# A hybrid attention and GLA layer: decays one head ahead, a modulation inside attention, a gate projection and the blocks of queries in other places

## The chip, the cores and the metric

The kernel runs on one core of a Trainium2 chip. The metric is the device time of one execution in microseconds (us). Several runs of the kernel are timed, and the profile is of one more execution. PE is the matrix engine, DVE, ACT and POOL are the vector, scalar and GpSimd engines, SP issues the transfers (DMA).

## The reference

One layer over 1024 latent tokens of width 1024 in fp32, with 256 context tokens. Cut to what matters:

```
h = modulate(rms_norm(x), shift1, scale1)          # adaLN: 6 vectors of 1024, silu(c) @ w_ada
k, v, gla k, gla v, low rank, q, gla q, gla gate, gate_a, gate_g = split(h @ w_in)
attention: 8 query heads, 2 key/value heads, qk norm, rotary, softmax over 1024 + 256 keys
g = log_sigmoid(lowrank @ w_gk + b) / 16           # decays, per head and direction
gla: S_t = diag(exp(g_t)) S_(t-1) + k_t^T v_t ;  o_t = q_t S_t    # forward and backward, 4 heads
y = sigmoid(gate_a) * (attn @ w1) + sigmoid(gate_g) * (gla @ w2)
x = x + gate1 * (y @ w_out)                        # gate1 is vector 2 of the six
out = x + gate2 * mlp(modulate(rms_norm(x), shift2, scale2))      # vectors 3, 4, 5
```

## The kernel before

Every large product is split into high and low parts and run as three matmuls (`mm3`, L171 to L175), so PE has most of the work. The program is a sequence of stages. Each is written as Python generators, and `merge(main, filler, n_main)` (L40) runs a main generator and fills it with the steps of projection GEMMs, spread evenly. A tile scheduler then sets each engine's order; each engine works its own queue in that order, and all transfers are issued from SP's one queue in order. Buffers come from rings: S 19, G 16, m1 10, m2 6, small ty 14.

The stages in time: a prologue (norm, the first two modulation vectors); `context()` (the 256 context tokens); `gla(0)` to `gla(3)`, each with projections as fillers; the projections of k and q for attention, where each one's norm, rotation and transposes (its *tail*, L850) is merged with the next one's GEMM; attention; the merge of the branches; the output projection; the MLP.

Within `gla(h)` come, in this order, the decays (`decays`, L435: four PSUM tiles of 512 columns, then Abs, Exp and Ln on ACT and subtractions on DVE), one cumulative scan per direction (L645, L647), the *level stage* (seven levels: differences of the scans at L673 and L674, L677 and L678, Exp at L675 and L679, multiplications by q and k at L683 and L685, 32-wide block products on PE at L631), a preparation, and the *chunk loop* (L722: eight steps i, two directions, where PE's L732 and L734 read and feed the state that DVE updates at L736).

`modulation()` (L1084) computes the other four modulation vectors from a 1024x4096 weight; `along` (L57) runs it step by step beside the fillers that are marked `M(...)` at L912 to L915:

```
for i in range(4):
    raw = self.m2(shape=(P, 2, 256))
    nc.sync.dma_start(raw, a["w_ada"][i * 256:(i + 1) * 256, c0:c0 + 256].rearrange("(k p) c -> p k c", p=P))
    for k in range(2):
        sk = self.silu[:, 2 * i + k, 0:1]
        if i == 0 and k == 0:
            nc.vector.tensor_scalar(acc, raw[:, k, :], sk, None, op0=ALU.mult)
        else:
            nc.vector.scalar_tensor_tensor(acc, raw[:, k, :], sk, acc, op0=ALU.mult, op1=ALU.add)
```

Attention (L954) goes over 16 blocks of 128 queries of one key/value group, four heads each. While a block's probabilities are transposed (L996), split by ACT (L190) and DVE (L191) and multiplied with the values (`values`, L1011), the next block's scores run (`scores`, L963), with maxima on DVE (L975 to L980) and exponentials on ACT (L987, L988). The first block's scores are merged with the last gate projection, `pg(1, 3)`, and with the last query tail (L1044 to L1052). `kv_load` (L929) loads the keys and values of a group, `q_load` (L940) the queries of a block.

## Time and profile before

| | |
|---|---|
| three runs | 2148.75, 2148.76, 2155.94 us; median 2148.76 us |
| profiled execution | 2144.9 us; span of the trace 2143.0 us |
| granted clock of PE, mean over the span | 0.980 of full speed |
| busy time over the span | PE 94%, DVE 69%, ACT 47%, POOL 30% |

The profiled execution is one of its own and not among the three runs. A busy share is an average over stages; which engine is waited for differs from stage to stage. Times in the trace are counted from the span's start. "Busy" of matmuls is modelled, and a granted clock below 1 in a stretch means that PE ran part of it at the lower of its two levels.

### The profile page before, as it was taken

To read this page: it belongs to the slowest core of one execution; us is meant where nothing else is said; L and a number is where in the kernel's file an instruction comes from. 1 tells how busy PE (TensorE), PEld (TensorE's weight loads), DVE (VectorE), ACT (ScalarE), POOL (GpSimd) and SP (SyncE) were. 2 spreads that over 40 slices of the span, in tenths; PEclk is the share of its full clock that TensorE was granted. 3 is DMA by queue.
4 is the path that set the end of the run, shared out by engine and by line. 5 is a ranking of instruction groups with operands and counts; after the bars stand their busy time and mean duration, and the time that the engine had idled before them with its cause. 6 is when DMAs were issued, how large, how long until landed. Compare 5 with 4: busy or idle time off the path is not lost.

```text
span 2143.0 us, 32673 instructions
## 1 busy us (share of the span) xinstructions
PE 2018.4 (94%) x12526; PEld 1688.6 (79%) x12526; DVE 1482.1 (69%) x2216; ACT 999.8 (47%) x1783; POOL 634.7 (30%) x408
## 2 busy tenths in 40 slices
PE   4999898998999999789999998999699999999999
PEld 2898687887878999578888776877588887788887
DVE  6533787769668578577777678857756547788784
ACT  3354545435254223266666544336555556344341
POOL 2100322322331222100000356202423235475470
PEclk9999999999999999999999999999899999999999
DMA  8243431331524323461111367664153547644441
GB/s 290 64 121 120 134 99 37 104 106 37 157 64 156 112 79 140 159 184 45 35 55 40 122 215 246 220 215 143 44 177 134 186 143 240 212 157 157 138 153 64
DMA packets 230140, 284.13 MB, mean 133 GB/s; under 512 B 19376, under 2 KB 156736, under 8 KB 229984
## 3 DMA queue, kind: packets, MB, share of 16 engines
q1 hardware_dynamic: 229920, 281.91, 40.5%
q8 instruction: 99, 1.62, 0.3%
q0 software_dynamic: 64, 0.13, 0.1%
q14 instruction: 57, 0.47, 0.1%
HBM read 200.18 MB, written 81.81 MB: 132 GB/s over the span
## 4 chain that ended last, share of the span: by engine, by line
PE 51%; DVE 4%; DMA 1%; issue 1%; ACT 1%; POOL 0%; SPq 0%; DVEq 0%; ACTq 0%; POOLq 0%
PE p L173 8%; PE p L175 8%; PE p L174 8%; PE g L175 5%; PE g L173 5%; PE g L174 5%; PE b L996 3%; PE b L173 2%; PE b L175 2%; PE b L174 2%; PE s L173 2%; PE s L175 1%; PE s L174 1%; DVE G L1155 1%; DVE W L1128 0%
## 5 line engine op out<-in xcount | busy, mean ns | idle before, releaser
L173 PE MATMUL g<-whi,S 128*128 128x256 f32 x896 | 259.9, 290 | 0.0
L175 PE MATMUL g<-whi,S 128*128 128x256 f32 x896 | 253.4, 283 | 0.0
L174 PE MATMUL g<-wlo,S 128*128 128x256 f32 x896 | 252.7, 282 | 0.0
L1128 DVE TENSOR_TENSOR W<-Q,W 128x512 fp32r<-128x512 f32 x160 | 130.9, 822 | 101.3 <-ACT W L1127 101.0
L173 PE MATMUL p<-S,W 128*128 128x512 f32 x384 | 155.1, 404 | 20.1 <-ACT W L1127 18.2
L173 PEld LDWEIGHTS g<-whi,S 128*128 128x128 f32 x896 | 170.9, 191 | 1.8 <-issue 0.4
L174 PEld LDWEIGHTS g<-wlo,S 128*128 128x128 f32 x896 | 170.9, 191 | 1.0
L175 PEld LDWEIGHTS g<-whi,S 128*128 128x128 f32 x896 | 170.6, 190 | 0.3
L1127 ACT CAST W<-R 128x512 fp32r<-128x512 f32 x152 | 93.9, 620 | 149.5 <-PE p L175 105.7
L161 POOL TENSOR_TENSOR wlo<-wraw,whi 128x1024 fp32r<-128x1024 f32 x32 | 92.8, 2918 | 232.9 <-ACT whi L160 231.5
L175 PE MATMUL p<-S,W 128*128 128x512 f32 x384 | 154.0, 402 | 2.0 <-DVE W L1128 2.0
L174 PE MATMUL p<-S,W 128*128 128x512 f32 x384 | 154.2, 402 | 0.0
L1128 DVE TENSOR_TENSOR W<-R,W 128x512 fp32r<-128x512 f32 x152 | 139.5, 921 | 21.2 <-ACT W L1127 21.1
L175 PE MATMUL p<-G,W 128*128 128x512 f32 x384 | 152.0, 396 | 0.1
L174 PE MATMUL p<-G,W 128*128 128x512 f32 x384 | 152.0, 396 | 0.0
L1175 POOL TENSOR_TENSOR Q<-R 128x512 f32<-128x512 f32 x40 | 60.3, 1509 | 309.5 <-DVE W L1128 214.8
L173 PE MATMUL p<-G,W 128*128 128x512 f32 x384 | 151.9, 396 | 0.0
L1127 ACT CAST W<-Q 128x512 fp32r<-128x512 f32 x160 | 98.5, 621 | 110.7 <-PE g L175 51.1
L191 DVE TENSOR_TENSOR G<-b,G 128x512 fp32r<-128x512 f32 x164 | 111.8, 686 | 48.0 <-ACT G L190 47.7
L173 PE MATMUL g<-S,whi 128*128 128x512 f32 x336 | 139.0, 414 | 6.0 <-ACT S L268 6.0
L175 PE MATMUL g<-S,wlo 128*128 128x512 f32 x336 | 135.1, 402 | 0.8 <-POOL wlo L161 0.8
L1155 POOL TENSOR_TENSOR S<-S 128x512 fp32r<-128x512 f32 x38 | 53.9, 1420 | 274.1 <-ACT S L1154 204.9
(339 smaller groups left out, 5561.7 us busy)
## 6 DMA issues: line engine op xcount, KB each, us to landing
R<-in_w_mlp_dram SPq DMA_DIRECT2D x32, 1024.0 KB, 6.2
wraw<-in_w_in_dram SPq DMA_DIRECT2D x60, 512.0 KB, 4.0
u<-S SPq DMA_DIRECT2D x96, 256.0 KB, 2.9
m<-in_w_ada_dram SPq DMA_DIRECT2D x64, 256.0 KB, 4.2
G<-u SPq DMA_DIRECT2D x64, 256.0 KB, 3.8
S<-u SPq DMA_DIRECT2D x48, 256.0 KB, 3.6
G<-in_w_ada_dram SPq DMA_DIRECT2D x16, 512.0 KB, 10.5
R<-in_w_out_dram SPq DMA_DIRECT2D x8, 1024.0 KB, 7.4
```

The lines of the kernel that those rows point to most:

```text
L161: self.lo_engine.tensor_tensor(lo[:, s, :], raw, hi[:, s, :].bitcast(F32), op=ALU.subtract)
L173: nc.tensor.matmul(out, lh, rh, start=first, stop=False, skip_group_check=more)
L174: nc.tensor.matmul(out, lh, rl, start=False, stop=False, skip_group_check=more)
L175: nc.tensor.matmul(out, ll, rh, start=False, stop=last, skip_group_check=more)
L191: self.nc.vector.tensor_tensor(lo, src, hi.bitcast(F32), op=ALU.subtract)
L996: nc.tensor.transpose(pt[:, h * P:(h + 1) * P], src, self.ident)
L1127: self.nc.scalar.copy(hi, v)
L1128: self.nc.vector.tensor_tensor(lo, v, hi.bitcast(F32), op=ALU.subtract)
L1155: (engine or self.nc.vector).tensor_tensor(b[:, 1, :], v, b[:, 0, :].bitcast(F32), op=ALU.subtract)
L1175: tt(s[0], a21, a22, op=ALU.add)
```

## The change

- `decays` becomes a generator that stops after each of its four tiles. A new `sums_of_decays(h)` runs it and scans in place. Head h+1's is stepped from head h's chunk loop, from i=2 on; head 0's is at the end of `context()`. `gla(h)` only fetches the result.
- `modulation()` leaves the fillers and is stepped once for each block of attention from the second on. It now loads 32 tiles of 128x1024 into S buffers, multiplies them on ACT (`scalar.mul`) and adds them on POOL, where before it took 128 operations of 128x256 on DVE and 64 loads.
- `pg(1, 3)` is merged with the last query tail, ahead of attention, whose first scores now run alone.
- The blocks of queries are taken in another order, and the loads of the second group, of the modulation and of the GLA outputs are issued behind the latest `q_load` (`issue_after`). The PSUM pool of attention takes over its banks tile by tile.

The diff, cut:

```diff
                 nc.vector.tensor_scalar(mn, p, bias, 0.0, op0=ALU.add, op1=ALU.min)
                 todo.append((s, mn))
+                yield
         for s, _ in todo:
             nc.scalar.activation(s, s, AF.Exp, scale=-1.0)
         for s, mn in todo:
             nc.scalar.activation(s, s, AF.Ln, bias=1.0)
             nc.vector.tensor_tensor(s, mn, s, op=ALU.subtract)
+        yield
...
-
-    CONTEXT_STEPS = 1 + 2 + 4 * 6 + 2 + 1
+        yield from self.sums_of_decays(0)
+
+    CONTEXT_STEPS = 1 + 2 + 4 * 6 + 2 + 1 + 7
...
-        b = []
-        gs = [self.G(), self.G()]
-        self.decays(h, self.lr, T, gs)
-        yield
...
-                nc.vector.tensor_tensor_scan(bt[:, ::-1], self.reset, g[:, ::-1], 0.0, op0=ALU.mult, op1=ALU.add)
-            b.append(bt)
-            yield
-        bf, bb = b
+        bf, bb = b = self.b.pop(h)
...
+        ahead = self.sums_of_decays(h + 1) if h < 3 else None
...
+                if h < 3 and i >= 2:
+                    next(ahead, None)
                 yield
         nc.vector.tensor_scalar(ss, ss, 1.0 / 256, EPS, op0=ALU.mult, op1=ALU.add)
         self.orstd[h] = self.rsqrt(ss, NT)
         self.o[h] = o
         yield
 
-    GLA_STEPS = 2 + 3 + 21 + 1 + 6 + 16 + 1
+    GLA_STEPS = 2 + 21 + 1 + 6 + 16 + 1
+
+    def sums_of_decays(self, h):
+
+        nc = self.nc
+        self.b[h] = b = [self.G(), self.G()]
+        yield from self.decays(h, self.lr, T, b)
+        for d in range(2):
+            r = slice(None, None, -1 if d else 1)
+            nc.vector.tensor_tensor_scan(b[d][:, r], self.reset, b[d][:, r], 0.0, op0=ALU.mult, op1=ALU.add)
+            yield
...
-            pg, md = self.proj_gate, self.modulation()
+            pg = self.proj_gate
...
-            M = lambda f: along(f, md, 6)
             merge(self.context(), [(4, lambda: self.fm_block(w1, 1, sink)), gv(0), pg(0, 1), pg(1, 2)], self.CONTEXT_STEPS)
...
-            merge(self.gla(0), [kq(1), pg(0, 2), M(gv(1))], self.GLA_STEPS)
-            merge(self.gla(1), [kq(2), go(0), pg(0, 3), M(gv(2))], self.GLA_STEPS)
-            merge(self.gla(2), [kq(3), go(1), pg(1, 0), M(gv(3))], self.GLA_STEPS)
-            merge(self.gla(3), [pg(1, 1), go(2), M(self.proj_v())], self.GLA_STEPS)
+            merge(self.gla(0), [kq(1), pg(0, 2), gv(1)], self.GLA_STEPS)
+            merge(self.gla(1), [kq(2), go(0), pg(0, 3), gv(2)], self.GLA_STEPS)
+            merge(self.gla(2), [kq(3), go(1), pg(1, 0), gv(3)], self.GLA_STEPS)
+            merge(self.gla(3), [pg(1, 1), go(2), self.proj_v()], self.GLA_STEPS)
...
                 merge(tail, [gemm], 10)
                 tail = nxt[1]() if nxt else iter(())
-            run_all(md)
+            merge(tail, [pg(1, 3)], 10)
             self.attention_loads()
-        return tail, pg(1, 3)
...
         for j in range(2):
-            self.move(q[j], self.qT[j][4 * kv:4 * kv + 4, :, qb * P:(qb + 1) * P].rearrange("h d t -> d h t"))
+            self.last_q = self.move(q[j], self.qT[j][4 * kv:4 * kv + 4, :, qb * P:(qb + 1) * P].rearrange("h d t -> d h t"))
...
+    def attention(self):
+        nc = self.nc
+        with self.psum_phase("pat", {"s": 2, "sc": 1, "b": 3}, "tile") as self.pp:
...
-                th = qb // 4
-                self.at[kv, th] = rb
-                if kv == 1:
-                    if th == 0:
-                        return
+                at = self.at.setdefault(qb % 4, {})
+                at[kv, qb // 4] = rb
+                if len(at) == 4:
                     t0 = qb % 4 * P
                     for t in range(2):
-                        self.operands(self.at, t, lambda i: self.atD[:, i, :, t0:t0 + P].rearrange("j d t -> d j t"), lambda r: r.rearrange("p (h t) -> p h t", t=P))
-
-            blocks = [(kv, q + 4 * th) for q in range(4) for kv in range(2) for th in range(2)]
+                        self.operands(at, t, lambda i: self.atD[:, i, :, t0:t0 + P].rearrange("j d t -> d j t"), lambda r: r.rearrange("p (h t) -> p h t", t=P))
+
+
+            blocks = [(0, 0), (0, 4), (0, 1), (1, 0), (1, 4), (0, 5), (1, 1), (1, 5)] + [(kv, q + 4 * th) for q in (2, 3) for kv in range(2) for th in range(2)]
...
-            def first():
-                for _ in scores(0, st):
-                    if st["todo"]:
-                        exponentials(st)
-                    next(tail, None)
-                    yield
-                run_all(tail)
-            self.lo_engine = nc.vector
-            merge(first(), [gate], 12)
+            for _ in scores(0, st):
+                if st["todo"]:
+                    exponentials(st)
+            if st["todo"]:
+                exponentials(st)
             self.close_wts.close()
             self.wts, self.close_wts = self.open("tw", side="right", reuse_waits="tile")
-            late = []
+            late, md = [], self.modulation()
             for n, (kv, qb) in enumerate(blocks):
                 nxt, sg = None, iter(())
-                if n == 0:
-                    kvs[1] = self.kv_load(1)
-                if n in (9, 11):
-                    self.load_blocks(self.glaD, n // 11)
                 if n + 1 < len(blocks):
                     nxt = start(n + 1)
                     sg = scores(blocks[n + 1][0], nxt)
+                with self.tc.issue_after(self.last_q.ins):
+                    if n == 0:
+                        kvs[1] = self.kv_load(1)
+                    if n > 0:
+                        next(md, None)
+                    if n in (9, 11):
+                        self.load_blocks(self.glaD, n // 11)
...
-            accs = []
-            for j in range(4):
-                c0 = (2 + v) * D + j * 256
-                acc = self.m1()
-                for i in range(4):
-                    raw = self.m2(shape=(P, 2, 256))
-                    nc.sync.dma_start(raw, a["w_ada"][i * 256:(i + 1) * 256, c0:c0 + 256].rearrange("(k p) c -> p k c", p=P))
-                    for k in range(2):
-                        sk = self.silu[:, 2 * i + k, 0:1]
-                        if i == 0 and k == 0:
-                            nc.vector.tensor_scalar(acc, raw[:, k, :], sk, None, op0=ALU.mult)
-                        else:
-                            nc.vector.scalar_tensor_tensor(acc, raw[:, k, :], sk, acc, op0=ALU.mult, op1=ALU.add)
-                accs.append(acc)
...
+            acc = self.S()
+            for k in range(KT):
+                raw = self.S()
+                nc.sync.dma_start(raw, a["w_ada"][k * P:(k + 1) * P, (2 + v) * D:(3 + v) * D])
+                sk = self.silu[:, k, 0:1]
+                if k == 0:
+                    nc.scalar.mul(acc, raw, sk)
+                else:
+                    nc.scalar.mul(raw, raw, sk)
+                    nc.gpsimd.tensor_tensor(acc, acc, raw, op=ALU.add)
+                if k % 4 == 3:
+                    yield
             p = self.ps("a")[:, :256]
             for j in range(4):
-                nc.tensor.matmul(p[32 * j:32 * j + 32, :], self.ones[:, 0:32], accs[j], start=True, stop=True, tile_position=(0, 32 * j))
+                nc.tensor.matmul(p[32 * j:32 * j + 32, :], self.ones[:, 0:32], acc[:, j * 256:(j + 1) * 256], start=True, stop=True, tile_position=(0, 32 * j))
             row = self.m1()
```

What it moves on three engines is shown as rows of each engine's order (line, operation, written tile, read tiles, shape; `a` and `g` are PSUM tiles, a number tells buffers of one name apart).

ACT in head 0, the decays of head 1 before: they stand together, after the chunk loop (L742 is its last operation).

```order
L448 ACTIVATE G_3151<-a_3153,vec 128x512
L448 ACTIVATE G_3151<-a_3159,vec 128x512
L448 ACTIVATE G_3152<-a_3165,vec 128x512
L448 ACTIVATE G_3152<-a_3171,vec 128x512
L453 ACTIVATE G_3151<-G_3151 128x512 x2
L453 ACTIVATE G_3152<-G_3152 128x512 x2
L455 ACT_TABLE_LOAD
L455 ACTIVATE G_3151<-G_3151 128x512 x2
L455 ACTIVATE G_3152<-G_3152 128x512 x2
```

All Exps run ahead of all Lns here, so one table load separates them.

ACT at the same decays after, inside head 0's chunk loop (L719 is the chunk loop's copy, L438 Abs, L444 Exp, L446 Ln). Exp and Ln alternate tile by tile, with a table load at each alternation; head 0's copies stand between them. Over the program the table loads grow from 17 to 35.

```order
L438 ACTIVATE G_2752<-a_2754,vec 128x512
L719 COPY G_2654<-a_2745 128x256
L444 ACTIVATE G_2752<-G_2752 128x512
L438 ACTIVATE G_2752<-a_2766,vec 128x512
L446 ACT_TABLE_LOAD
L446 ACTIVATE G_2752<-G_2752 128x512
L719 COPY G_2655<-a_2760 128x256
L444 ACT_TABLE_LOAD
L444 ACTIVATE G_2752<-G_2752 128x512
L446 ACT_TABLE_LOAD
L446 ACTIVATE G_2752<-G_2752 128x512
L438 ACTIVATE G_2753<-a_2804,vec 128x512
```

DVE at that place after (L440 is the bias and minimum, L447 the subtraction that takes Ln's result, L741 the scans, L717 the update of the state that the chunk loop's matmuls read).

```order
L447 TENSOR_TENSOR G_2752<-m_344_2758,G_2752 128x512
L447 TENSOR_TENSOR G_2752<-m_348_2770,G_2752 128x512
L717 SCALAR_TENSOR_TENSOR m_351_2801<-m_340_2749,ty_2564,a_2797 128x256
L741 SCALAR_TENSOR_TENSOR G_2752<-reset,G_2752 128x1024
L440 TENSOR_SCALAR m_353_2808<-a_2804,vec 128x512
L717 SCALAR_TENSOR_TENSOR m_355_2813<-m_346_2763,ty_2602,a_2810 128x256
L440 TENSOR_SCALAR m_357_2820<-a_2816,vec 128x512
L447 TENSOR_TENSOR G_2753<-m_353_2808,G_2753 128x512
L447 TENSOR_TENSOR G_2753<-m_357_2820,G_2753 128x512
L741 SCALAR_TENSOR_TENSOR G_2753<-reset,G_2753 128x1024
L717 SCALAR_TENSOR_TENSOR m_359_2851<-m_351_2801,ty_2564,a_2847 128x256
```

The updates of the state, which had stood among filler work, now stand between subtractions and scans; `m_359`, the state after step i=4 in one direction, is behind the second scan.

SP at the start of attention before (`q_hi` and `q_lo<-G` are the last query tail's stores, `G<-k_hi` begins `kv_load(0)`, `S_8984<-k_lo` is in `kv_load(1)`, `sgg<-S` are the last gate's stores, `S<-q_hi` the second block's queries).

```order
L122 DMA q_hi<-G_8626 128x1024
L122 DMA q_lo<-G_8627 128x1024
L122 DMA G_8690<-k_hi 128x1024
L122 DMA q_hi<-G_8669 128x1024
L122 DMA q_lo<-G_8670 128x1024
L122 DMA G_8691<-k_lo 128x1024
...
L605 DMA sgg<-S_8887 128x1024
L122 DMA S_8984<-k_lo 128x1024
...
L122 DMA S_8986<-v1l 128x4x128
L122 DMA S_8993<-q_hi 128x4x128
```

The first group's keys stand between the tail's stores, and the second block's queries last.

SP at the same place after.

```order
L112 DMA q_hi<-G_8521 128x1024
L112 DMA q_lo<-G_8522 128x1024
L598 DMA sgg<-S_8506 128x1024
L112 DMA q_hi<-G_8554 128x1024
L112 DMA q_lo<-G_8555 128x1024
L112 DMA G_8575<-k_hi 128x1024
L112 DMA G_8576<-k_lo 128x1024
...
L112 DMA G_8578<-v1l 128x4x128
L112 DMA S_8671<-q_hi 128x4x128
L112 DMA S_8671<-q_lo 128x4x128
L112 DMA S_8674<-k_hi 128x1024
```

The first group's loads went behind all of the tail's stores and the gate's, and the second block's queries went ahead of the second group's keys (`S_8674`).

## Rows read from the trace of the kernel before

**Rows 1.** The page, part 1: busy time, share and instructions.

```profile
PE 2018.4 (94%) x12526; PEld 1688.6 (79%) x12526; DVE 1482.1 (69%) x2216; ACT 999.8 (47%) x1783; POOL 634.7 (30%) x408
```

**Rows 2.** Stretches: length, busy PE, PEld, DVE, ACT, POOL, granted clock, DMA, GB/s.

```profile
240.00:300.00 60.00, 51.86 (x613) 41.34 (x612) 53.76 (x58) 32.15 (x42) 19.56 (x11) 0.91 0.23 73
355.00:405.00 50.00, 43.81 (x673) 39.43 (x672) 49.03 (x62) 26.50 (x36) 13.41 (x8) 0.97 0.14 43
485.00:530.00 45.00, 38.76 (x582) 35.91 (x583) 42.89 (x55) 20.57 (x27) 10.84 (x7) 0.92 0.12 37
615.00:655.00 40.00, 33.76 (x540) 30.47 (x538) 40.00 (x46) 18.26 (x24) 15.97 (x7) 0.96 0.17 54
...
850.00:940.00 90.00, 69.49 (x354) 54.98 (x354) 51.59 (x97) 33.45 (x70) 11.04 (x8) 0.92 0.67 199
...
940.00:1200.00 260.00, 260.00 (x1506) 216.78 (x1504) 197.79 (x406) 177.06 (x385) 21.97 (x17) 1.00 0.14 43
...
370.00:380.00 10.00, 5.88 (x97) 5.61 (x96) 10.00 (x10) 3.07 (x4) 5.04 (x2) 0.83 0.36 107
```

**Rows 3.** Waits: us in total, times, longest (240 to 700; last row 850 to 940).

```profile
PE a L631 <- DVE G L685: 26.2, 12, 5.1
...
PE a L732 <- DVE m L736: 5.8, 5, 2.5
...
PE s L173 <- DMA S<-q_hi: 6.2, 1, 6.2
```

**Rows 4.** DVE's timeline, second head: start, us, instruction, [idle before <- releaser].

```profile
350.02 2.50 DVE L456 TENSOR_TENSOR G<-m,G 128x512 f32<-128x512 f32 x4 [2.93 <-ACT G L455]
...
354.64 2.77 DVE L647 TENSOR_TENSOR_SCAN G<-reset,G 128x1024 f32<-128x1024 uint8 x1
...
369.74 3.10 DVE L683 TENSOR_TENSOR G<-G,G 128x1024 f32<-128x1024 f32 x1
372.76 3.36 DVE L685 TENSOR_TENSOR G<-G,G 128x1024 f32<-128x1024 f32 x1
...
381.31 1.21 DVE L685 TENSOR_TENSOR G<-G,G 128x1024 f32<-128x1024 f32 x1
```

**Rows 5.** ACT's timeline, first head's end and second head's decays.

```profile
319.86 0.37 ACT L738 COPY G<-a 128x256 f32<-128x256 f32 x1 [2.92 <-DVE m L736]
...
342.87 1.84 ACT L448 ACTIVATE G<-a,vec 128x512 f32<-128x512 f32 x3
...
345.86 2.18 ACT L453 ACTIVATE G<-G 128x512 f32<-128x512 f32 x4
348.06 1.28 ACT L455 ACT_TABLE_LOAD   x1
349.36 2.20 ACT L455 ACTIVATE G<-G 128x512 f32<-128x512 f32 x4
```

**Rows 6.** PE's timeline, two successive steps of the first head's chunk loop.

```profile
314.89 0.67 PE L732 MATMUL a<-m,G 128*128 128x256 f32 x2
...
319.98 0.67 PE L732 MATMUL a<-m,G 128*128 128x256 f32 x2
```

**Rows 7.** Groups by line (240 to 700; L1009 950 to 1200; L675 whole span).

```profile
L736 DVE SCALAR_TENSOR_TENSOR m<-m,ty,a 128x256 f32<-128x256 f32 x53 | 25.1, 477 | 44.7 <-PE a L734 38.3 <-DMA m<-in_w_ada_dram 6.3
...
L1009 ACT COPY m<-b 128x512 f32<-128x512 f32 x13 | 7.7, 593 | 0.9 <-PE b L1007 0.9
...
L675 ACT ACTIVATE G<-G 128x1024 f32<-128x1024 f32 x28 | 29.7, 1061 | 58.4 <-DVE G L674 58.4
```

**Rows 8.** Timelines of PE and of SP's queue at the start of attention.

```profile
887.08 0.58 PE L173 MATMUL sc<-S,S 128*128 128x256 f32 x1 [6.14 <-ACT m L987]
...
895.77 0.38 SPq L122 DMA_DIRECT2D q_hi<-G  x1
```

**Rows 9.** Transfers issued from 850 to 868: KB each, us to landing.

```profile
G<-k_lo SPq DMA_DIRECT2D x1, 512.0 KB, 6.0
```

**Rows 10.** Timelines of POOL and DVE in attention, two rows at one time.

```profile
996.79 1.29 POOL L803 TENSOR_TENSOR m<-m,m 128x512 f32<-128x512 f32 x1 [3.96 <-DVE m L1024]
...
996.89 0.68 DVE L191 TENSOR_TENSOR G<-b,G 128x512 fp32r<-128x512 f32 x1
```

## What the change does to the time: the prediction

> **What bounds the kernel now.** The page comes first: PE is busy 94% of a span of 2143.0 us [rows 1], so a gain has to come out of the 125 us in which PE idles, or out of stretches in which its clock is below full. Which of those the change touches is read from the table of stretches. The reader is to see three places. In the level stage of each of the four GLA heads (exponentials of decay sums, 32-wide block products at L631) PE is short of the length by 8.1, 6.2, 6.2 and 6.2 us, 26.8 together, at granted clocks of 0.91 to 0.97 [rows 2]. Between the last projections and steady attention (850 to 940 us) it is short by 20.5 us at 0.92, and in steady attention (940 to 1200) it is never idle at clock 1.00 [rows 2]; there nothing can be gained, and whatever delays PE's suppliers can be lost. The list of waits then names who is late: in the level stage PE's L631 waits for DVE's L685, 26.2 us in 12 waits, and in the chunk loop L732 waits for the state update L736, 5.8 us in 5 waits [rows 3].
>
> Why is DVE late in the level stage? Its timeline shows it packed: the scan L647 takes 2.77 us, and L683 and L685, normally 1.21, once took 3.10 and 3.36 [rows 4]. In the 10 us around those two, DVE is busy all the time, POOL 5.04 us, PE 5.88 [rows 2]. So there are two causes: work at the head of the stage (decays, four subtractions, two scans), and POOL's splitting of weights, which slows DVE.
>
> **Term A, decays and scans leave the head of the level stage.** Per head DVE loses there the two scans (5.5) and four subtractions of 0.62 (2.50 for four) [rows 4], some 8 us with the bias-and-minimum operations not counted, more than the 6.2 to 8.1 that PE idles. The part that stays is POOL's: 3.10 + 3.36 - 2x1.21 = 4.0 us in each of three heads, 12 in all. DVE will come to it with a lead, which the ring of 16 G buffers limits; I keep 7.5 of the 12. So 26.8 - 7.5 = 19.3 are gained. Clock: 60x0.09 + 50x0.03 + 45x0.08 (third) + 40x0.04 = 12 us of full speed are missing in the four stretches, about half of it inside idle time; of the other 6 I count 5 as gained. **A = -24** (bounds -33, all of it, and -15, all of POOL's 12 staying and half of the clock).
>
> **Term B, the same work in the chunk loop of the head before.** It lands between state updates, on ACT's and DVE's queues in the order printed ahead. For head 0, ACT from the first Abs to the last Ln of head 1's decays: 4 Abs of 0.61, 4 Exp of 0.55, 4 Ln of 0.55, 4 copies of 0.37, and 7 table loads of 1.28 (one before) = 2.4 + 2.2 + 2.2 + 1.5 + 9.0 = 17.3 us [rows 5]. A step of two directions' five matmuls and 24 of filler takes 5.1 us [rows 6]. The first Abs follows the first pair of step i=2, an estimated 1.8 us into it, so the last Ln ends at 19.1. On DVE the subtraction (0.62), a scan (2.77) and then the state update (0.48 [rows 7]) stand behind it in order, to 23.0. PE wants that state at the start of step i=5, three steps on: 5.1 each, two of them lengthened by the decays' own matmuls to an estimated 6.1, 17.3 in all. It stalls about 6 us. For heads 1 and 2, whose steps carry more filler and whose orders hold five loads, I take 1 each. A stall brings some clock with it: the level stretches lost 6 us of clock outside their 26.8 of idle (above), so 0.22 x 8 = 1.8 here, and **B = +10** (bounds 0, if the compiled order lets DVE pass; +20, if heads 1 and 2 stall as head 0 does). The scans run in place, so nothing else of them is new. Head 0's own decays go to the end of the context stage, where PE has its fillers; no cost taken, since they were run there too, only 8 us later; uncovered they would cost those 8.
>
> The Trainium skill ("ScalarE: Activation LUTs", section "What ACT_TABLE_LOAD costs") states that a switch costs 1283 ns of load and about 1380 ns of drain. The rows agree with the load alone: the Exps end at 348.04, the load is at 348.06 for 1.28, the first Ln starts at 349.36 [rows 5], so 1.3 per switch, and by the page's 2.66 the seven would take 9.7 us more. The rows decide; it is a rival below.
>
> **Term C, the second modulation leaves DVE in the chunk loops.** 128 operations of 128x256 disappear from the queue in which L736 stands. What PE can get back is at most the 5.8 us of its waits there [rows 3]; **C = -4** (0 to -5.8).
>
> **Term D, start of attention.** Before, PE waits 6.1 us for the first heads' exponentials [rows 8] and 6.2 for a q load [rows 3] that stood in SP's queue behind the key and value loads of the second group and the gate's store, the rest in small pieces: 20.5 idle, and 90x0.08 = 7.2 of clock [rows 2], half of it inside the idle; 24 to be had. After, PE has no gate GEMM beside the first scores, and in SP the first K load stands behind the last q stores and the gate's store instead of ahead of them (the order ahead). Before, such a store was issued at 895.77 [rows 8] (DVE then ran the scores' maxima too); without them I take 885 for the K load. It lands 6.0 later [rows 9], at 891. PE reached the same amount of work at 880.9 before (887.1 minus its 6.1 of wait), say 883 now. So 7.5 idle for the load, 2 and 3 for the first two heads' exponentials that nothing covers, 2 of clock, 1.5 of the small pieces: 16. **D = -8** (bounds: K at 875, -16; K as late as 895.8, +4). This second group's load behind the next block's q load takes away the 6.2.
>
> **Term E, ACT in attention.** ACT is busy 177 of 260 us there [rows 2]; 13 blocks in 250 us make 19.2 per block [rows 7], of which ACT has 13.1. Of the 32 multiplies of 128x1024, 25 stand within 15 heads' exponentials in ACT's order, or 6.7 per block over 3.75 blocks; at 1.06 each (L675, same engine and shape [rows 7]) 7.1 more: 20.2 against 19.2, a loss of 1.0 x 3.75 = 3.8. Some will stand ahead of a cast that PE waits for; 2 more. **E = +6** (bounds 0, all in ACT's free 6.1; +34, 32x1.06 all on the path). The POOL adds find POOL idle, 22 of 260 us busy [rows 2]. Would they hold DVE as the weight splits do? DVE's L191, with an input in PSUM, ran 0.68 under a POOL addition that began 0.1 before it [rows 10]; the slowed L683 and L685 had SBUF inputs only. Nothing taken.
>
> **Term F.** The modulation's small product takes one of three "b" PSUM buffers four times; at most a wait of one cast each: **+1** (0 to 4).
>
> **Sum:** -24 + 10 - 4 - 8 + 6 + 1 = -19 against the profiled 2144.9, 2125.9. The profiled execution lay 3.9 below the median of the runs, 2148.76, so 2129 or 2130 for the median; I say 2129.
>
> **Rivals.** (1) The first K load comes early and the chunk loop doesn't stall: D -16, B 0, E as said, so -37 and 2112; with C whole 2110. For it speaks that the last projection's norm now has a whole GEMM beside it; against, SP's order. (2) POOL keeps DVE at it: the splits fall on the levels wherever DVE stands, and A is only -12, the sum -7: 2142. For it: 3.10 and 3.36 against 1.21. Against: DVE's lead. Beside this, the Trainium skill ("SBUF — State Buffer", section "Who interferes with whom") has VectorE and GpSimd share a port pair that one locks; the two slowed rows agree, L191's does not suffer by it. (3) The other side: every multiply falls on PE's path, since ACT's casts feed PE in each of 10 steps per block and ACT is in order. E is then +34, the sum +9, 2158: slower. It decides from E = 25, 0.78 us lost per multiply. For it: PE idles 0 there, and ACT's casts are already waited for by DVE; against: ACT idles 83 of 260 us. (4) Each table switch costs its load and a drain of the same size: head 0 stalls 15 rather than 6, heads 1 and 2 about 5 each, B +29, the sum 0, 2149. That is the page's rule in "ScalarE: Activation LUTs" of the Trainium skill; the 0.02 us before the load speak against. (5) The change does not do what it says, since DVE was late for the exponentials of the levels themselves: A is -7, the sum -2, 2147.
>
> **How the numbers follow.** Forecast (2114 to 2139) 0.55; (1) 0.14; (2) 0.10; (3) 0.10; (4) 0.05; (5) 0.06. The range leaves out (3) and half of (1): 2108 to 2150. A measurement here tells 0.5%, 10.7 us, from no change: faster is below 2138.0, slower above 2159.5. Faster: 0.53 + 0.14 + 0.03 = 0.70. Slower: half of (3), with bounds of B on top, and little else, 0.07. Same: 0.23.
>
> **What would show it.** A: L631's waits for L685 fall from 26.2 to under 10, all behind slowed DVE rows, and the stretches of the levels get a clock over 0.97. B: one wait of some 6 us in head 0 of the chunk matmul that reads L717's state, behind table loads 1.3 apart. C: no wait for modulation. D: PE short by some 13 us at the start of attention, most of it before the first score, released by the K load. E: attention's first five blocks with modulation at 20 rather than 19.2 us, PE's transposes and value products waiting for ACT. I am wrong if E passes 25, if the chunk loop stalls in all three heads, or if L631 waits as before.

## The result, and the profile after

| | before | changed |
|---|---|---|
| median of four runs | 2148.76 us | 2132.01 us (2128.25 to 2132.9) |
| ratio to before, 95% interval | | 0.9913 (0.99 to 0.9926) |
| profiled execution, span | 2144.9, 2143.0 us | 2132.9, 2131.1 us |

The change made the kernel faster by 0.9%, 16.7 us between the medians and 12.0 us between the two profiled executions, to which the rows below belong. The prediction said 2129 us.

The page of the changed kernel, part 1 (to be read against [rows 1]): PE did the same work, in a span 12 us shorter. PE's idle time went from 124.6 us to 112.5, all of the difference.

```profile
PE 2018.6 (95%) x12526; PEld 1685.4 (79%) x12526; DVE 1432.7 (67%) x2088; ACT 1053.9 (49%) x1833; POOL 675.8 (32%) x436
```

Stretches of the changed kernel, columns as in [rows 2]: first the context stage, then the four heads' level stages, head 0's chunk loop, the start of attention, the rest of attention, and the blocks that hold the modulation.

```profile
0.00:241.00 241.00, 208.32 (x1258) 174.03 (x1258) 122.80 (x211) 110.05 (x164) 35.62 (x35) 0.97 0.46 145
240.00:300.00 60.00, 54.55 (x684) 42.70 (x683) 51.23 (x55) 30.00 (x39) 19.18 (x12) 0.97 0.19 59
350.00:410.00 60.00, 57.65 (x795) 50.06 (x794) 52.59 (x62) 28.88 (x39) 20.34 (x13) 0.99 0.22 63
474.00:534.00 60.00, 57.62 (x793) 49.97 (x792) 53.09 (x62) 28.69 (x39) 20.35 (x13) 0.98 0.22 63
598.00:655.00 57.00, 56.88 (x810) 50.30 (x809) 47.25 (x67) 29.44 (x44) 15.28 (x10) 1.00 0.23 71
300.00:346.00 46.00, 40.07 (x252) 36.52 (x252) 18.62 (x31) 25.66 (x45) 5.74 (x3) 0.96 0.12 35
855.00:940.00 85.00, 71.46 (x378) 55.66 (x378) 54.60 (x105) 57.85 (x109) 34.42 (x16) 0.94 0.90 290
940.00:1198.00 258.00, 247.22 (x1437) 200.89 (x1435) 191.97 (x380) 184.32 (x381) 57.99 (x33) 1.00 0.29 85
...
880.00:1060.00 180.00, 165.45 (x946) 132.79 (x946) 137.65 (x262) 144.40 (x281) 78.26 (x37) 1.00 0.54 167
```

The context stage of the kernel before, not shown ahead, for comparison:

```profile
0.00:230.00 230.00, 200.75 (x1250) 168.38 (x1250) 114.05 (x201) 95.27 (x144) 34.88 (x36) 0.99 0.46 147
```

PE's waits in the changed kernel, whole span (us in total, times, longest), the rows that answer to [rows 3] and [rows 8] and two new ones. L624 is the block product (L631 before), L713 the chunk loop's state matmul (L732 before), L163 a score, L491 a matmul of the context stage, L759 a transpose in the projection of the GLA output gate, a filler that ends in the level stages of heads 1 and 2.

```profile
PE s L163 <- DMA G<-k_hi: 8.4, 1, 8.4
...
PE a L713 <- DVE m L717: 5.9, 2, 4.7
PE a L491 <- DVE G L486: 5.9, 2, 3.3
...
PE a L759 <- DVE m L777: 4.5, 4, 1.8
...
PE a L624 <- DVE G L665: 3.2, 3, 1.5
PE a L624 <- DVE G L663: 2.2, 1, 2.2
```

The reader is to see that the level stage is mostly settled: L624's waits for DVE went from 26.2 us to 5.4, all of them in head 0; in the last head PE lacks 0.1 us of 57. In heads 1 and 2 the transposes L759 wait 4.5 us for DVE instead (0.3 before). The chunk loop waits as long as before (5.9 against 5.8 us), but in head 0 alone. The start of attention lacks 13.5 us where it lacked 20.5. Two stages lost. The context stage has 3.4 us more idle time (32.7 against 29.3) and about 5 us less clock (241x0.03 against 230x0.01), and attention after 940 us has 10.8 us of idle time where it had 0.2 (940 to 1209 us of the kernel before).

The waits at L759 show POOL holding DVE. Two of DVE's L777 take 0.88 us together elsewhere in this stage (386.43, 390.54); here they took 3.19 and ended just after POOL's weight splits (L151), and PE stood 1.83 us for them. In head 2 the same three rows come again, with a wait of 1.83 us at 531.94.

```profile
402.99 4.88 POOL L151 TENSOR_TENSOR wlo<-wraw,whi 128x1024 fp32r<-128x1024 f32 x2 [7.85 <-issue]
404.96 3.19 DVE L777 SCALAR_TENSOR_TENSOR m<-G,ty,m 128x256 f32<-128x256 f32 x2
408.21 0.55 PE L759 MATMUL a<-ident,m 128*128 128x128 f32 x3 [1.83 <-DVE m L777]
```

The chunk loop's stall is where it was forecast. ACT's and then DVE's timeline of the changed kernel at the end of head 1's decays (L444 Exp, L446 Ln, L447 subtraction, L741 scan, L717 state), then PE's.

```profile
325.07 0.63 ACT L446 ACTIVATE G<-G 128x512 f32<-128x512 f32 x1
325.73 1.28 ACT L444 ACT_TABLE_LOAD   x1
327.02 0.63 ACT L444 ACTIVATE G<-G 128x512 f32<-128x512 f32 x1
327.56 0.35 ACT L719 COPY G<-a 128x256 f32<-128x256 f32 x1
327.93 1.28 ACT L446 ACT_TABLE_LOAD   x1
329.22 0.63 ACT L446 ACTIVATE G<-G 128x512 f32<-128x512 f32 x1
```

```profile
329.89 0.69 DVE L447 TENSOR_TENSOR G<-m,G 128x512 f32<-128x512 f32 x1 [3.45 <-ACT G L446]
330.61 2.29 DVE L741 TENSOR_TENSOR_SCAN G<-reset,G 128x1024 f32<-128x1024 uint8 x1
332.82 0.45 DVE L717 SCALAR_TENSOR_TENSOR m<-m,ty,a 128x256 f32<-128x256 f32 x1
```

```profile
324.13 0.70 PE L713 MATMUL a<-m,G 128*128 128x256 f32 x2 [1.27 <-DVE m L717]
333.33 0.95 PE L713 MATMUL a<-m,G 128*128 128x256 f32 x2 [4.67 <-DVE m L717]
```

Each change between Exp and Ln costs 1.3 us, the load alone, as [rows 5] had it; DVE stands 3.45 us for the last Ln, and PE gets its state behind the scan.

### The profile page after: what moved, and what is told of

It reads as the page before. It is cut to its first block, busy times and chain, and to the rows that moved or that the text cites. A ratio compares the mean times of both kernels' runs of the same rounds, so it can differ in the third digit from the quotient of the medians.

```text
span 2131.1 us, 32578 instructions
## 1 busy us (share of the span) xinstructions
PE 2018.6 (95%) x12526; PEld 1685.4 (79%) x12526; DVE 1432.7 (67%) x2088; ACT 1053.9 (49%) x1833; POOL 675.8 (32%) x436
## 4 chain that ended last, share of the span: by engine, by line
PE 76%; DVE 11%; DMA 5%; ACT 3%; issue 3%; POOL 1%; SPq 1%; ACTq 0%; DVEq 0%; POOLq 0%
PE g L163 12%; PE g L165 12%; PE g L164 12%; PE p L165 7%; PE p L163 7%; PE p L164 7%; PE b L986 3%; PE b L165 1%; PE b L163 1%; PE b L164 1%; PE s L163 1%; DMA S<-in_w_ada_dram 1%; PE a L713 1%; PE s L164 1%; PE s L165 1%
## 5 line engine op out<-in xcount | busy, mean ns | idle before, releaser
L163 PE MATMUL g<-whi,S 128*128 128x256 f32 x896 | 259.5, 290 | 0.0
L163 PE MATMUL p<-S,W 128*128 128x512 f32 x384 | 156.2, 407 | 21.7 <-ACT W L1111 18.4
L163 PEld LDWEIGHTS g<-whi,S 128*128 128x128 f32 x896 | 169.3, 189 | 1.8
L163 PE MATMUL g<-S,whi 128*128 128x512 f32 x368 | 152.6, 415 | 5.2 <-ACT S L258 5.2
L151 POOL TENSOR_TENSOR wlo<-wraw,whi 128x1024 fp32r<-128x1024 f32 x32 | 81.8, 2571 | 234.7 <-ACT whi L150 219.0
L163 PE MATMUL p<-G,W 128*128 128x512 f32 x384 | 151.9, 395 | 0.0
L164 PE MATMUL g<-S,whi 128*128 128x512 f32 x368 | 148.0, 402 | 0.0
L165 PE MATMUL g<-S,wlo 128*128 128x512 f32 x368 | 147.6, 401 | 0.0
L181 DVE TENSOR_TENSOR G<-b,G 128x512 fp32r<-128x512 f32 x160 | 109.1, 685 | 41.7 <-ACT G L180 41.4
## 6 DMA issues: line engine op xcount, KB each, us to landing
G<-in_w_ada_dram SPq DMA_DIRECT2D x16, 512.0 KB, 10.6
```

The lines of the kernel that those rows point to most:

```text
L151: self.lo_engine.tensor_tensor(lo[:, s, :], raw, hi[:, s, :].bitcast(F32), op=ALU.subtract)
L163: nc.tensor.matmul(out, lh, rh, start=first, stop=False, skip_group_check=more)
L164: nc.tensor.matmul(out, lh, rl, start=False, stop=False, skip_group_check=more)
L165: nc.tensor.matmul(out, ll, rh, start=False, stop=last, skip_group_check=more)
L181: self.nc.vector.tensor_tensor(lo, src, hi.bitcast(F32), op=ALU.subtract)
```

## The experiments

All kernels below compute the whole layer. Each was timed in five rounds against the kernel before; to tell it from the changed kernel, compare its ratio with 0.9913 (0.99 to 0.9926).

### Ln behind the last Exp

```diff
         for s, _ in todo:
-            nc.scalar.activation(s, s, AF.Exp, scale=-1.0)
-        for s, mn in todo:
-            nc.scalar.activation(s, s, AF.Ln, bias=1.0)
-            nc.vector.tensor_tensor(s, mn, s, op=ALU.subtract)
+            last = nc.scalar.activation(s, s, AF.Exp, scale=-1.0)
+        with self.tc.issue_after(last.ins):
+            for s, mn in todo:
+                nc.scalar.activation(s, s, AF.Ln, bias=1.0)
+                nc.vector.tensor_tensor(s, mn, s, op=ALU.subtract)
```

> The changed kernel with the decays' Ln instructions ordered behind the last Exp, so that each head has one or two table loads and the program 17 in place of 35. Theory: the chunk loop's stall in head 0 (5.9 us in two waits, L713 for L717) comes from the seven loads between Exp and Ln. Then it falls to 1 us or less, the clock of that stretch goes back to 1.00, and the time falls by 5 to 8 us, ratio 0.988 or 0.989. Rival: the stall comes from DVE's two scans and four subtractions ahead of the state's update, whatever ACT does; with all Lns at the end they even come in one piece, and the waits stay at 4 us or more, ratio 0.990 to 0.992.

Measured: 2117.32 us, ratio 0.9857 (0.9843 to 0.9872). Head 0's chunk loop in this kernel, as a stretch, then ACT and DVE in it (L447 is Ln here, L742 the scans):

```profile
300.00:346.00 46.00, 46.00 (x355) 42.14 (x354) 24.99 (x48) 21.16 (x46) 8.80 (x5) 1.00 0.15 47
```

```profile
317.18 1.28 ACT L447 ACT_TABLE_LOAD   x1
318.47 0.63 ACT L447 ACTIVATE G<-G 128x512 f32<-128x512 f32 x1
319.48 1.67 ACT L447 ACTIVATE G<-G 128x512 f32<-128x512 f32 x3
...
323.00 4.47 DVE L742 TENSOR_TENSOR_SCAN G<-reset,G 128x1024 f32<-128x1024 uint8 x2
```

The stall is gone and the clock is back at 1.00. The rival falls: both scans and four subtractions still run on DVE between state updates, the scans even in one piece of 4.47 us, and PE does not wait for them. The loads between Exp and Ln, and the places behind late Lns that they forced on DVE's subtractions and scans, were the stall; the edit changes both together. The gain is 0.0056, some 12 us, more than the 5 to 8 expected; the context stage, which runs head 0's decays in the same way, waited 1.2 us less (L492 for DVE 4.7 where L491 had 5.9), and the clock of head 0's level stage (241 to 300 us) went from 0.97 to 1.00. The rest of the gain was not taken apart.

### The first group's loads ahead of the last gate projection

```diff
-            merge(tail, [pg(1, 3)], 10)
             self.attention_loads()
+            merge(tail, [pg(1, 3)], 10)
```

> The changed kernel with the first group's keys, values and queries loaded ahead of the last gate projection and the last query tail, not behind them. Theory: the 8.4 us that PE waits for the key load ahead of the first score (issued at 864.2, landed near 870) are the order of SP's queue; they go, the first heads' exponentials still cost 2 to 4 us, and the time falls by 6 to 8 us, ratio 0.988. Rival: the first scores then wait for something that was late too (their PSUM banks, the last tail's work on DVE), or the tail waits for G buffers that the loads took early: less than 3 us are gained, ratio 0.990 or more.

Measured: 2120.89 us, 0.9877 (0.9863 to 0.989). The key load is issued at 833.4, where the changed kernel issued it at 864.2, and the wait of 8.4 us for it is in this kernel's list no more; the start of attention lacks 6.9 us, not 13.5, at full clock:

```profile
833.44 0.53 SPq L112 DMA_DIRECT2D G<-k_hi  x1
```

```profile
855.00:940.00 85.00, 78.13 (x436) 60.92 (x435) 60.51 (x117) 69.98 (x133) 40.99 (x19) 1.00 0.87 286
```

So this wait was the order of SP's queue. (This kernel's first scores run some 11 us earlier, so its window takes in more of steady attention.) What the first scores wait for next is small (0.5 us each).

### Where attention lost: loads a step ahead

```diff
-            for k in range(KT):
-                raw = self.S()
-                nc.sync.dma_start(raw, a["w_ada"][k * P:(k + 1) * P, (2 + v) * D:(3 + v) * D])
...
+            for k0 in (0, 4):
+                raws = [self.S() for _ in range(4)]
+                for k in range(k0, k0 + 4):
+                    nc.sync.dma_start(raws[k - k0], a["w_ada"][k * P:(k + 1) * P, (2 + v) * D:(3 + v) * D])
+                yield
+                for k in range(k0, k0 + 4):
...
```

> The changed kernel with each four loads of the second modulation issued one step (about one block) ahead of their four multiplications; nothing else differs, ACT has the same 32 multiplications. Theory: attention lost its 11 us (PE idle 10.8 us from 940 us to the end of attention, where before it was 0.2) because ACT, in order, stands at a multiplication whose weights have not landed, and the casts behind it come late; the ACT rows that wait for the modulation's transfers add up to some 11 us. Then PE's idle time there falls below 4 us and the ratio to the kernel before from 0.991 to 0.987 or 0.988 (some 2122 to 2125 us). Rival: ACT simply has too much work in these blocks (20.2 us of work in 19.2, as forecast); then the idle time stays at 8 us or more and the ratio at 0.990 to 0.992.

Measured: 2132.02 us, 0.9921 (0.9907 to 0.9935): no gain that shows. Its runs spread from 2126.98 to 2134.2, and the profiled one is the fastest of them. In that one ACT's waits for the modulation's weights fell from 10.9 us (8.6 and 2.3, below) to 3.2, and PE's idle time in the window below from 14.6 us to 6.4; PE's waits at 1000 to 1040 us, where the changed kernel's ACT stands at late weights, are gone, and most of those ahead of 960 us are not. From 940 us to the end of attention 6.1 us are left, between the 4 of the theory and the 8 of the rival. As for the time, the experiment is inconclusive; it says that late weights are not all of it.

What the rest is, the traces show, and neither the theory nor the rival has it. L993 adds the sums of a block, a DVE addition of 128x4 with both inputs in SBUF. The first line is the kernel before (L1003 there), the second the changed kernel; the figures are shortest, median and longest in ns.

```profile
L1003 DVE TENSOR_TENSOR ty<-ty x16: 149/152/161, 919.7 to 1200.9; 128x4 f32<-128x4 f32 x16
L993 DVE TENSOR_TENSOR ty<-ty x16: 149/153/2270, 890.3 to 1188.2; 128x4 f32<-128x4 f32 x16
```

Five of the sixteen took 0.98 to 2.27 us: they were held, that is, each lasted until an operation on POOL ended. Four were held by the modulation's additions (L1086), the one at 1014.48 by a subtraction of the attention outputs (L794) that had stood behind two of them in POOL's order. One of the five, with POOL's additions (four of 2.45 us, so one ends at 912.44) and PE's wait:

```profile
905.09 9.80 POOL L1086 TENSOR_TENSOR S<-S,S 128x1024 f32<-128x1024 f32 x4 [0.68 <-ACT S L1085]
910.19 2.27 DVE L993 TENSOR_TENSOR ty<-ty 128x4 f32<-128x4 f32 x1
913.40 0.62 PE L997 MATMUL b<-ident,ty 128*128 128x128 f32 x4 [1.71 <-DVE G L181]
```

PE's waits right behind the five, and behind one split of the GLA outputs held in the same way (L1139 on DVE, 2.12 us at 1040.32, 0.68 when free), are 1.71, 0.57, 1.65, 1.01, 2.00 and 1.23 us: 8.2 of the 14.6 between 880 and 1060 us, and 5.9 of the 10.8 after 940. The waits behind ACT with its late multiplications are 2.15, 0.53, 0.73 and 0.97: 4.4. So by these rows POOL's additions, by holding DVE, cost PE more than ACT's order did. With the loads a step ahead the waits behind ACT are nearly gone, and three of the held sums (2.06, 1.12 and 1.08 us) still cost PE 3.1 us in this window. This split is read from the rows; no run has the multiplications on ACT without the additions on POOL.

ACT's groups of multiplications in the changed kernel, 855 to 1200 us, and one of its rows:

```profile
L1085 ACT ACTIVATE S<-S,silu 128x1024 f32<-128x1024 f32 x28 | 32.8, 1185 | 8.6 <-DMA S<-in_w_ada_dram 8.6
L1083 ACT ACTIVATE S<-S,silu 128x1024 f32<-128x1024 f32 x4 | 4.6, 1157 | 2.3 <-DMA S<-in_w_ada_dram 2.3
```

```profile
1015.53 1.15 ACT L1085 ACTIVATE S<-S,silu 128x1024 f32<-128x1024 f32 x1 [2.02 <-DMA S<-in_w_ada_dram]
```

The stretch of the kernel with loads a step ahead:

```profile
880.00:1060.00 180.00, 173.58 (x996) 139.90 (x997) 136.99 (x274) 145.64 (x286) 63.62 (x31) 1.00 0.49 154
```

### One multiplication behind each head's exponentials

```diff
                     if nxt and nxt["todo"]:
                         exponentials(nxt)
+                        if n > 0:
+                            with self.tc.issue_after(self.last_q.ins), self.tc.issue_after(self.last_exp.ins):
+                                next(md, None)
...
+        for i in range(4 * KT + 3):
+            if i < 4 * KT:
...
+                if i + 3 < 4 * KT:
+                    load(i + 3)
...
+            if i % KT == 2 and i > KT:
+                product(i // KT - 1)
+            yield
```

> The changed kernel with the 32 multiplications of the second modulation put one behind each head's exponentials from the second block on, four to a block (ACT's order then has 13.1 + 4 x 1.16 = 17.7 us in a block of 19.2), each weight tile loaded three multiplications ahead, and the small product two multiplications late. In the changed kernel PE idles 14.5 us between 880 and 1060 us, in two places: up to 960 us with ACT busy 18 of 20 us, and at 1000 to 1040 us with ACT waiting for weights. Theory: both come from ACT's order. Then that idle time falls below 4 us, and the ratio to the kernel before from 0.9913 to 0.986 or 0.987. Rival: POOL's additions, 67 us of them, or DVE, which splits the GLA outputs in these blocks as well, make it; then 10 us or more stay, ratio 0.990 or more.

Measured: 2121.42 us, 0.9885 (0.9869 to 0.9902). The stretch, to be read against the last of the changed kernel's:

```profile
880.00:1060.00 180.00, 175.14 (x1003) 139.49 (x1003) 138.84 (x274) 147.23 (x290) 75.86 (x36) 1.00 0.55 171
```

PE's idle time falls from 14.6 us to 4.9, with about as much POOL and DVE work in the window (75.9 and 138.8 us against 78.3 and 137.7), and no ACT row waits for the modulation's weights any more. That misses the 4 us of the theory and is far from the rival's 10. But the edit spreads POOL's additions too: they follow the multiplications and stand one by one instead of in bunches of up to four. Only one of DVE's sums is still held for long (2.16 us at 968.73, and PE waits 1.70 behind it). So this run does not tell ACT's order from POOL's additions; spreading both is what paid. The ratio is 0.0015 above what was expected, and its interval just touches the changed kernel's.

### The multiplications on POOL

```diff
-                    nc.scalar.mul(acc, raw, sk)
+                    nc.gpsimd.tensor_scalar(acc, raw, sk, None, op0=ALU.mult)
...
-                    nc.scalar.mul(raw, raw, sk)
+                    nc.gpsimd.tensor_scalar(raw, raw, sk, None, op0=ALU.mult)
```

> The changed kernel with the 32 multiplications of the second modulation on POOL in place of ACT. Both theories of attention's loss (ACT waiting for late weights, ACT overfull) have ACT's casts on time then: PE idle from 940 us to the end of attention below 2 us, ratio 0.986 to 0.988. Third theory: the loss comes from POOL's additions, which hold DVE, or from the transfers; with twice the work on POOL it stays at 10 us or grows, ratio 0.991 or more.

Measured: 2203.93 us, 1.0258 (1.0244 to 1.0272), 72 us slower than the changed kernel. It tells nothing about the two theories, and something else instead. Waits of this kernel, 900 to 1080 us, all engines:

```profile
PE b L986 <- DVE G L181: 58.1, 3, 52.5
ACT S L1138 <- POOL S L1085: 53.6, 2, 48.9
DVE S L1139 <- ACT S L1138: 52.0, 2, 48.0
```

A multiplication takes POOL 2.85 to 2.89 us where ACT took 1.17. L1138 and L1139, which split GLA's outputs for the merge, take S buffers from the ring in which the weight tiles lie. ACT stands 48.9 us at L1138 until POOL has used up a tile, DVE stands behind ACT at L1139, and the attention splits behind both (L181) starve PE. The ring passes POOL's delay to two engines that have no part in the modulation.

### The modulation on DVE again, beside the GLA heads

```diff
-            merge(self.gla(0), [kq(1), pg(0, 2), gv(1)], self.GLA_STEPS)
+            merge(self.gla(0), [kq(1), pg(0, 2), M(gv(1))], self.GLA_STEPS)
...
-                    if n > 0:
-                        next(md, None)
```

> The changed kernel with the second modulation back as it was before (on DVE in 128x256 pieces beside the GLA heads' projections); decays, gate projection and block order stay as changed. It measures what the move of the modulation alone is worth. By my accounting it lost 11 us in attention and gained 4 to 6 in the chunk loops: undone, PE idles below 4 us in attention after the first block, its waits for the state's update grow from 5.9 to about 12 us, and the ratio is 0.988 to 0.990. Rival: with scans and subtractions now in DVE's chunk loops, DVE cannot take the modulation there as well; the waits in chunk loops grow by 15 us or more, ratio 0.994 or more.

Measured: 2130.05 us, 0.9928 (0.9915 to 0.9941). The ratio is above the 0.988 to 0.990 that was expected, and its interval leaves them out; it overlaps the changed kernel's and just touches the rival's 0.994. The waits moved as said: attention from 940 us on lacks 0.2 us, and the chunk loops wait 9.6 us for the state and 3.1 for a copy, where the changed kernel waits 5.9. Two rows of this kernel's waits (L722, L723, L727 and L729 are its chunk loop):

```profile
PE a L723 <- DVE m L727: 9.6, 6, 3.7
...
PE a L722 <- ACT G L729: 3.1, 1, 3.1
```

The modulation's move by itself was worth nothing that can be told from zero: it gave back in attention what it saved in the chunk loops.

### The decays back, all of them and head 0's alone

```diff
-        yield from self.sums_of_decays(0)
...
+        for _ in self.sums_of_decays(h):
+            pass
...
-        ahead = self.sums_of_decays(h + 1) if h < 3 else None
...
-                if h < 3 and i >= 2:
-                    next(ahead, None)
```

> The changed kernel with each head's decays and scans back at the head of its own GLA stage, head 0's too; the rest stays as changed. By my accounting the move gained some 25 us in the level stages and lost 8 in head 0's chunk loop and 8 in the context stage (3.4 of idle and 5 of clock there): undone, L624's waits for DVE are back at 20 us or more, L713's fall below 2, and the ratio is 0.994 to 0.996. Rival: the level stages got faster because the modulation left DVE, not because the decays did; then L624 still waits less than 10 us and the ratio is 0.988 to 0.991.

Measured: 2137.37 us, 0.996 (0.9947 to 0.9973), and L624's counterpart waits for DVE again (this kernel's row):

```profile
PE a L623 <- DVE G L669: 24.6, 12, 4.8
```

The modulation was off DVE here, so the level stage's waits come from the decays and scans at its head. No matmul of the chunk loops waits for the state in this kernel. The move of the decays was worth 0.0047, some 10 us net.

With head 0's decays alone back in `gla(0)`:

> The changed kernel with head 0's decays alone back at the head of its own stage; those of heads 1 to 3 stay one head ahead. Theory: at the end of the context stage they cost what they cost at the head of head 0, since the context stage got 3.4 us more idle and 5 us less clock there: ratio within 0.002 of 0.9913. Rival: the context stage hides them (that part of its loss has another cause), and undone they show in head 0's level stage: 0.994 or more.

Measured: 2128.9 us, 0.9923 (0.991 to 0.9937), 0.001 from the changed kernel. The idle time that the context stage lost is that of head 0's decays (of the clock, 0.98 came back, where the kernel before had 0.99), and their place makes no difference that shows: 0 to 241 us now lacks 29.4 us instead of 32.7, and 241 to 300 us 6.9 instead of 5.5 at a clock of 0.94 instead of 0.97, and 300 to 346 us 8.7 instead of 5.9: 45.0 in all against 44.1.

### The edits together

Ln order and early loads together:

> The changed kernel with two of the edits measured alone: Ln behind the last Exp (0.9857) and the first group's loads ahead of the last gate projection (0.9877), beside 0.9913 for the changed kernel. If the two take away waits at different places, as their traces say (chunk loop of head 0; first score), the gains add: 0.9913 - 0.0056 - 0.0036 = 0.982. Rival: the time taken out at one place comes back as waits in attention, whose second to fourth blocks ACT bounds: 0.985 or more.

Measured: 2110.33 us, 0.983 (0.9813 to 0.9848).

These two with one multiplication behind each head's exponentials:

> The same with one multiplication behind each head's exponentials as well (0.9885 alone): if all three add, 0.982 - 0.003 = 0.979, some 2102 us against 2147 of the kernel before. Rival: as for the two edits, 0.983 or more.

Measured: 2098.27 us, 0.9772 (0.9759 to 0.9785), the fastest of all. Its head 0's chunk loop and its start of attention, which begins 23 us earlier here (first score at 846.9 us, in the changed kernel at 870.4):

```profile
300.00:346.00 46.00, 46.00 (x348) 41.81 (x347) 26.53 (x49) 22.21 (x47) 7.25 (x4) 1.00 0.15 46
830.00:915.00 85.00, 81.60 (x439) 65.22 (x438) 65.39 (x123) 55.76 (x116) 22.51 (x13) 1.00 0.68 223
```

The two edits with the modulation on DVE beside the GLA heads:

> The two edits (Ln order, early loads) with the second modulation on DVE in the GLA heads as before. The modulation's move alone came out even (0.9928 undone against 0.9913), because it paid in attention what it saved in the chunk loops. With the table loads gone from the chunk loop the modulation should cost less there, since DVE no longer gets its Ln results late: 0.981 to 0.983, level with the first of these three. Rival: DVE itself is full in the chunk loops: 0.985 or more.

Measured: 2113.71 us, 0.9844 (0.983 to 0.9857), a little above what was expected, and not to be told from the first of the three. So the gains add: three sites, each with its own wait. Spread out, the multiplications and additions gave 0.0058 here and 0.0028 alone; the intervals don't tell these two apart.

## Why the prediction was right, step by step

- **Term A (-24)** held in its mechanism, by the row that it named: L631's waits went from 26.2 us to 5.4, and the level stretches' missing clock from 12 us to 3.6. Undone it brought the waits back (24.6). Its size was too hopeful: PE's idle time in these stretches fell by 16.8 us, where 19.3 and 5 of clock were forecast. What is left there is POOL's, as forecast, but more than the 7.5 us kept. Of L624's 5.4, all in head 0, 2.2 stand right behind an L663 that a split held (3.40 us at 272.18, 1.22 when free) and 1.5 behind held rows at 242.33 to 245.87; the other 1.7 were not taken apart. The transposes L759 add 4.5 in heads 1 and 2, most of it behind an L777 held in the same way. Only the slowed rows that DVE's lead covers cost nothing (L665 took 3.09 us in the second head, at 379.77, and no PE wait follows). The bound of -15 is a slip: 26.8 less 12 and half of the 5 make 17.
- **Term B (+10)** held for head 0: forecast 6 us of stall, measured 4.67 and 1.27, behind loads 1.3 apart, with 1.8 us of clock. Heads 1 and 2 don't stall; 1 each was taken. Rival 4, a drain of a load's size at each switch, falls: the loads stand 1.3 us apart from the next activation, as in [rows 5]. The Trainium skill's 2.66 per switch ("ScalarE: Activation LUTs", section "What ACT_TABLE_LOAD costs") is not what these rows show. The Trainium skill's rule to batch by set (same title, section "Table sets: the hidden batching unit") fits the Ln experiment, which put the Exps together and the Lns behind them, and it paid. The Trainium skill's section also lists a set with both exp and ln, which would need one load for the two; here every change between them had its load.
- **Term C (-4)**: no wait in the chunk loops has the modulation behind it, and outside head 0's decays none is left, so 5.8 us went. With the decays back and the modulation off DVE none was left at all; with the modulation back on DVE, 12.7 us of waits against 5.9 say 6.8.
- **Term D (-8)**: 20.5 to 13.5 us idle, so -7, with 7.2 to 5.1 of clock. The wait for the key load was 8.4, forecast 7.5; issue (864.2) and PE's arrival (862.0) were both some 21 us earlier than the 885 and 883 taken, and only their difference held. Of the 13.5, 2.3 belong to term E.
- **Term E (+6)** was mis-sized: 10.6 us in attention after 940 us, and 2.3 before. The forecast counted ACT's work by blocks (20.2 us in 19.2). It left out that ACT, in order, would stand at multiplications whose weights had not landed (10.9 us in the changed kernel). And where it asked whether POOL's additions would hold DVE, "Nothing taken" was wrong: it had looked at L191, with an input in PSUM, and not at the block sums, with both inputs in SBUF. Five of those were held, and PE waited 8.2 us behind them and a held split, 5.9 of it after 940. Rival 3 (+34) was not near.
- **Term F (+1)** doesn't show: PE's list has no wait of the small product for a buffer.
- **The term taken as nothing** was wrong: head 0's decays at the end of the context stage. "Uncovered they would cost those 8" is near what happened, 3.4 us of idle and some 5 of clock by the rounded clock of the two rows.

How the terms add up is read from idle time alone, since PE's busy time is the same in both kernels (2018.4 and 2018.6 us, at a mean clock of 0.980 and 0.981), so that over the whole span the clock gave nothing that shows. PE's idle time changed by +3.4 us up to 241 us, by -16.8 in the four level stretches (241 to 300, 346 to 410, 474 to 534, 598 to 660) and +1.6 in the chunk loops between them, by -3.0 from 660 to 850, -7.0 from 850 to 940, +10.6 from there to the end of attention and -0.9 behind it. That makes -12, the 12.0 measured between the two profiled executions.

Set against it, the forecast of -19 had A too large by 7, D by 1, E too small by 5 and the context stage by 3, while B, C and F together came out at -1.4 where +7 was forecast, a stall in head 0 that the other chunk loops' lost waits made good. So errors of 16 one way and of 9 the other met in a sum that is 7 off. That the predicted 2129 lies only 3 us from the measured 2132 is luck on top: the medians are 16.7 apart where the profiled executions are 12.0, since the profiled run of the changed kernel was its slowest and that of the kernel before lay 3.9 below its median.

## What to carry to other kernels

Work moved off a late engine's path has to be priced in its new place with that engine's order as compiled: here the same decays took 1 table load at one place and 7 at another, and one ordering edge gave back more than the stall that the trace showed. An in-order engine that takes on a multiplication also takes on the wait for its operand, so spread such work behind instructions that come at a steady pace, and load ahead. Before a slower engine gets the work, look at who else draws from the ring of its buffers, and at which short operations of another engine will run beside it: here a sum of 0.15 us was held for up to 2.27.

## What the runs showed of the hardware

- Abs and Copy stand between Exp and Ln in ACT's order without a table load of their own; a change between Exp and Ln costs 1.28 us of load and nothing more that the rows show.
- POOL took 2.85 to 2.89 us for a 128x1024 multiplication by a column and 2.39 for an addition, ACT 1.17 for the same multiplication.
- DVE's 128x4 addition with both inputs in SBUF took 0.15 us, and 0.98 to 2.27 in five places beside an operation on POOL, ending with it; DVE's L181, with an input in PSUM, kept its mean of 0.68 us over the same stretch.
- The stall in head 0's chunk loop took its clock with it (0.96 over 46 us), and when the stall was gone the stretch had 1.00.
